# Two-layer flow backbone on one core: convolutions placed behind their columns, output sums read from PSUM, and VectorE kept in emission order through the global attention

## The chip, the cores and the metric

The kernel runs on one core of one Trainium2 chip. The metric is the device time of one execution in microseconds (us). A core has five engines that each work through a queue of their own: TensorE (PE; matmuls and, as PEld, their weight loads), VectorE (DVE), ScalarE (ACT), GpSimd (POOL) and SyncE (SP, which here only starts DMAs). Matmul results go to PSUM, in eight banks of 128 partitions x 2 KB; everything else on the chip lies in SBUF.

## The reference, cut to what matters

Two transformer-like layers run over 2048 latent tokens and 256 context tokens of width 1024. Each layer normalises (RMS, with shift and scale from a conditioning vector), projects to 3328 columns, mixes, multiplies by SiLU gates and projects back into the residual. All of it is float32.

```python
x = x + gate[:, None] * jnp.matmul(y, w_out[layer])
```

Layer 0 has two branches. Branch a is global attention with 8 heads over all 2304 keys:

```python
sc = jnp.einsum('bqkgd,bnkd->bkgqn', q_blk, k_all) * scale
p = jax.nn.softmax(sc, axis=-1)
o = jnp.einsum('bkgqn,bnkd->bqkgd', p, v_all)
```

Branch b is the Hyena operator: a short convolution of 3 taps over three parts of 512 channels, then twice a long convolution (through transforms of length 4096) times the next part:

```python
z = parts[0]
for o in range(HYENA_ORDER):
    z = parts[o + 1] * bidir_long_conv(z, filt[:, o, 0], filt[:, o, 1], d_skip[o])
```

The context tokens pass through the same weights and attend to themselves. Layer 1 has windowed attention (with a sink) and 2-D neighbourhood attention in place of the two branches. The output is the latent stream after layer 1.

## The kernel before

**How the order comes about.** The program is written as one long Python function, `kern`. Its instructions are handed to a scheduler that knows what each one reads and writes and that plays the program through with estimated durations; on each engine it takes, among the instructions that are ready in that play, the one written (emitted) first. The order found there is fixed in the queues, and on the chip each engine follows it strictly. Within `tc.manual_schedule(engines={...})` (L1474) the named engines keep the order of emission instead. Before, this held for TensorE alone in the global attention. Tiles come from pools: tiles of one tag share a ring of `bufs` slots, and a new tile waits until the slot's last user is through. A pool that is opened where another was closed waits for the tiles of the old one that lie in its memory.

**Precision.** A float32 product is made of three fast matmuls: both operands are split into a high part (`hi`) and the rest (`lo`), and `mm3` (L216) adds hi x hi, hi x lo and lo x hi. `load_w` (L229) loads a weight matrix in tiles of 128x512 (`wraw`, a ring of 3), has ScalarE cast each to `whi` (L242) and GpSimd subtract it to `wlo` (L243).

**Layer 0, first half (0 to about 1140 us).** The filters of Hyena and the modulation sums are made, and the tokens go through in three groups (`GRP`, L175): `ln0` normalises a group, `kvq` makes keys, values and queries, `us((b,))` makes column block b of the Hyena input for all three parts b (`cols`, evicted by VectorE at L341 and stored to `u0`), and `gates` the gate columns. The modulation of layer 0's gate and of layer 1 (`ada_sum`, L86, matmuls at L95) runs beside the second and third group and sums into three PSUM tiles of tag `x`, a ring of 3. In the third group stand, in this order: `us((0, 1))`, `conv(0)`, `us((2,))`, `conv(1)`, the first gate block, `gate_convs`, `kvq` and the second gate block with the first maxima. `conv(part)` calls `latent_conv` (L700): the short convolution of a part (VectorE at L725 and L726), transposes (L737), and for part 0 the first stage of the long convolution (matmuls at L668 and L669 into tiles of tag `x`).

**Global attention (about 1140 to 2255 us), `glob_attn` (L907).** 16 units (4 query blocks x 4 head pairs) of 9 batches, each batch 2 key tiles x 2 heads. A batch emits scores (L979, L980, exponentials on ScalarE at L981 into `Pt`, a ring of 5), then the products with the values of the batch before (L998) into one PSUM bank, and then GpSimd's running sum of probabilities (`pacc`, L993). Spread among the scores are the maxima of the coming unit: `max_step` emits a matmul (L892) into a bank of tag `m`, a ring of 3, and VectorE's reduction of it (L893); the 41st step of a unit, `max_fin`, collects them (L939, L943) and sends them by DMA into the queries. When a unit's last batch is through, `finish` (L1000) loads the gate (`agt`), sums the denominators (L1007), has ScalarE copy them (`rec`, L1009) and hands back six small steps, one of which follows each later score: four reciprocals of a quarter each (VectorE, L1012), two products on GpSimd (L1015, L1016) and `finish_y` (L365), which splits the result into `yhi` (ScalarE, L369) and `ylo` (L370) and stores both to `yT`.

**What else runs in it.** `hooks(b)` gives every batch further steps. Batches 0 to 109 carry the Hyena steps (`hyena_steps`, L754): for both orders 32 frequency steps and 16 inverse steps; the inverse step of order 0 multiplies in PSUM on VectorE, casts on ScalarE (L838) and subtracts on VectorE (L839). The very last step, in one piece, is 16 calls of `finish_y` on the result `yb` (L857 on), alternating between GpSimd and VectorE for the subtraction, with `yhi` and `ylo` both in the ring of 3 tiles of tag `hev`. At batch 110 the Hyena pools are closed and the pools of the output projection opened in their memory (`out_pools`, L1362); from batch 125 on one output job per batch follows (18 jobs; `job` in `out_jobs`, L1391). A job loads weights if it is the first of its half, loads `oy` (y transposed, hi and lo, rings of 2), loads `x` (`ox`, L1417 and L1419; 6 tiles in the first group), makes 24 matmuls (`pso`), multiplies them by the gate into the tile `ot` (L1425) and adds that to x (L1426). The context rows of modulation and the gate are handled the same way.

**Layer 1.** The attention's pools are closed (`stG`) and those of layer 1's projections opened on the same side (`hT1`, `s1`). For each of the three groups come the output jobs that are left, `norm` (transposes L302, activation L305 into `lnh`, L306 and L307), and `rows` and `cols`: window keys and values, window q, neighbourhood k and q, neighbourhood v, gates. In the third group `window_keys` (L1440) loads the keys and values of the window attention for all tokens (`wk1`, `wk2`, `wvt`, 4.5 MB) and its mask right behind the window q rows. Then come layer 1's attention (about 3080 to 3680 us) and the last output projection.

The two lines of a job that the change rewrites, and the call under the manual order:

```python
t = rg.tile([P, 512], F32, tag="bo", name="ot", bufs=3)
V.tensor_tensor(out=t, in0=po, in1=gate, op=ALU.mult)
V.tensor_tensor(out=x, in0=x, in1=t, op=ALU.add)
```

```python
with tc.manual_schedule(engines={mybir.EngineType.PE}):
    glob_attn(ga, gap, hooks, M0)
```

Of the kernel before, what the change touches and what calls it, by code (L numbers as in the profile page):

```python
# [9 lines left out]
F32 = mybir.dt.float32  # L10
# [30 lines left out]
def kern(ctx, tc, nc, I, C, out):  # L41
# [207 lines left out]
    class Proj:  # L249
# [98 lines left out]
        def ev_v(self, dst):  # L348
            def f(ps, tt):
                vt = self.rg.tile([P, 512], F32, tag="bo", name="vt", bufs=3)  # L350
                S.copy(vt, ps)
                nc.sync.dma_start(dst[tt], vt)
            return f
# [11 lines left out]
    def finish_y(sb, y, ft, t0, n, yT=yT, tags=("yhi", "ylo"), bufs=2, eng=None):  # L365

        hi = sb.tile([P, 512], F32R, tag=tags[0], name="yhi", bufs=bufs)
        lo = sb.tile([P, 512], F32R, tag=tags[1], name="ylo", bufs=bufs)
# [538 lines left out]
    def glob_attn(sb, ps, hooks, M0):  # L907
# [92 lines left out]
        def finish(n, yo, acc):  # L1000

            qb, hp = units[n]
            gt = sb.tile([P, 512], F32, tag="agt", name="agt", bufs=1)
# [4 lines left out]
            rec = sb.tile([P, 512], F32, tag="rec", name="rec", bufs=1)  # L1008
# [9 lines left out]
            return [lambda i=i: quarter(i) for i in range(0, 512, 128)] + [gate, lambda: finish_y(sb, yo, hp, qb * 512, 512, bufs=1, eng=G)]  # L1018
# [3 lines left out]
        acc, po, ended, last, pend = {}, {}, {}, None, []  # L1022
        total = 16 * 41
# [9 lines left out]
        for b in range(nb + 4):  # L1033
# [23 lines left out]
            if last is not None:  # L1057
# [5 lines left out]
                if ks == 16:  # L1063
                    yo = sb.tile([P, 512], F32, tag="yo", name="yo", bufs=2)
# [144 lines left out]
    with stS as st:  # L1209
# [109 lines left out]
        us((0, 1))  # L1319
# [6 lines left out]
        conv(0)  # L1326
        us((2,))
        conv(1)
# [52 lines left out]
    def out_jobs(g, halves, xs=None, early=()):  # L1381
# [9 lines left out]
        def job(b, i, tt, mm):  # L1391
            c = slice(512 * b, 512 * b + 512)
            rg, xo, gl = O0["rg"], O0["xo"], O0["gl"]
            if i == 0 and w_out.get("b") != b:
# [4 lines left out]
            ty = [xo.tile([P, 8, P], F32R, tag=f"oy{s}", name=f"oy{s}", bufs=2) for s in range(2)]  # L1399
            for s in range(2):  # L1400
                nc.sync.dma_start(ty[s].bitcast(F32), yT[s, :, :, tt * P:(tt + 1) * P].rearrange("f p t -> p f t"))
# [9 lines left out]
            else:  # L1411
                if len(xs) == i:
                    xt = xo.tile([P, 1024], F32, tag="lnx", name="ox", bufs=6)
                    if early:
# [9 lines left out]
            t = rg.tile([P, 512], F32, tag="bo", name="ot", bufs=3)  # L1424
            V.tensor_tensor(out=t, in0=po, in1=gate, op=ALU.mult)  # L1425
            V.tensor_tensor(out=x, in0=x, in1=t, op=ALU.add)  # L1426
# [13 lines left out]
    def window_keys():  # L1440
# [8 lines left out]
        wvt = aw.tile([P, 18, P], F32, tag="wv", name="wv")  # L1449
        for s in range(2):  # L1450
# [21 lines left out]

# [505 lines left out]
```

## Time and profile before

| what | value |
|---|---|
| median of 3 runs | 3856.79 us |
| lowest and highest | 3853.07 and 3857.14 us |
| the profiled execution's own time | 3855.73 us |
| its span, first to last instruction | 3854.0 us |
| mean granted TensorE clock | 0.975 |

The profile is one execution as the hardware profiler recorded it. Rows of the timeline give start, duration, engine, line, operation, output and inputs, shape and count, and in square brackets how long the engine was idle before and what it waited for. Rows that group a line's instructions give minimum, median and maximum in ns and the first and last start. Rows of the table by stretch give the busy time (and number of instructions) of each engine in a stretch, then the granted clock, the DMA share and GB/s; a table for one line names only that line's engine.

### The profile page before, as it was taken

How to read it: one execution, taken by the hardware profiler on the slowest of the kernel's cores; microseconds unless marked ns; L12 is line 12 of the kernel's file. 1: busy time of each engine (PE TensorE's matmuls, PEld its weight loads, DVE VectorE, ACT ScalarE, POOL GpSimd, SP SyncE). 2: the span in 40 equal slices, each digit the busy share in tenths (PEclk: the TensorE clock that was granted, in tenths of full speed). 3: DMA queues.
4: the chain of work that ended last, by engine and by line, in shares of the span. 5: the costliest groups of instructions: out<-in, count | busy, mean ns of one | idle time of the engine just before them, and what ended most of it. 6: DMA issues, size and time to landing. Idle time of an engine off the chain costs nothing.

```text
span 3854.0 us, 57179 instructions
## 1 busy us (share of the span) xinstructions
PE 3628.1 (94%) x20112; PEld 2607.1 (68%) x20112; DVE 2284.9 (59%) x4370; ACT 1784.9 (46%) x3480; POOL 1735.3 (45%) x1433
## 2 busy tenths in 40 slices
PE   6999999999779999999989989999999999999999
PEld 2788777666555544555545667778877888888887
DVE  5854862634967765776664348185168167677622
ACT  3644642423526655666452334344144266666610
POOL 1544642222447786777796554353244123222310
PEclk8999999999889999999999999999999999999999
DMA  6343445366666555443253545545566376365365
GB/s 195 118 140 123 133 133 141 114 224 219 203 191 189 172 162 173 123 148 110 91 197 96 146 148 152 164 152 155 157 175 169 118 171 147 90 151 135 113 178 169
DMA packets 537650, 586.23 MB, mean 152 GB/s; under 512 B 70590, under 2 KB 361720, under 8 KB 534290
## 3 DMA queue, kind: packets, MB, share of 16 engines
q1 hardware_dynamic: 521090, 551.10, 48.8%
q10 hardware_dynamic: 13856, 25.18, 1.8%
q0 software_dynamic: 2416, 6.29, 0.6%
q8 instruction: 159, 2.61, 0.3%
q14 instruction: 129, 1.06, 0.1%
HBM read 389.62 MB, written 192.75 MB: 151 GB/s over the span
## 4 chain that ended last, share of the span: by engine, by line
PE 69%; DVE 13%; issue 5%; DMA 5%; ACT 4%; POOL 2%; SPq 1%; ACTq 0%; DVEq 0%; POOLq 0%
PE psB L221 16%; PE pso L221 7%; PE po L998 6%; PE psA L221 5%; PE npt L1580 4%; PE no L1592 4%; PE pS L979 4%; PE pm L892 3%; PE pS L980 3%; PE ns L1561 2%; PE ns L1567 2%; DMA wraw<-in_w_in_dram 2%; PE hpX L806 1%; PE hpC L799 1%; PE hpH L811 1%
## 5 line engine op out<-in xcount | busy, mean ns | idle before, releaser
L243 POOL TENSOR_TENSOR wlo<-wraw,whi 128x512 fp32r<-128x512 f32 x368 | 494.4, 1357 | 784.9 <-ACT whi L242 529.3
L993 POOL TENSOR_TENSOR pacc<-pacc,Pt 128x512 f32<-128x512 f32 x512 | 647.1, 1286 | 191.4 <-ACT Pt L981 189.1
L221 PE MATMUL psB<-hT,whi 128*128 128x512 f32 (+1 forms) x2560 | 659.4, 346 | 3.9 <-DVE bo L341 3.5
L221 PE MATMUL psA<-whi,hT 128*128 128x512 f32 (+1 forms) x1952 | 574.8, 375 | 28.3 <-ACT vt L361 8.4
L893 DVE TENSOR_REDUCE mx<-pm 128x1 f32<-128x512 f32 (+1 forms) x640 | 389.1, 631 | 194.4 <-PE pm L892 190.1
L221 PEld LDWEIGHTS psB<-hT,whi 128*128 128x128 f32 x2560 | 445.1, 190 | 87.0 <-issue 23.9
L981 ACT ACTIVATE Pt<-pS 128x512 f32<-128x512 f32 x576 | 333.0, 597 | 352.5 <-PE pS L980 313.7
L221 PE MATMUL psB<-hT,wlo 128*128 128x512 f32 (+1 forms) x1280 | 433.8, 344 | 0.0
L221 PEld LDWEIGHTS psA<-whi,hT 128*128 128x128 f32 x1952 | 359.0, 194 | 98.7 <-ACT vt L361 11.7
L242 ACT CAST whi<-wraw 128x512 fp32r<-128x512 f32 x368 | 222.2, 618 | 301.4 <-DMA wraw<-in_w_in_dram 119.5
L221 PE MATMUL psA<-wlo,hT 128*128 128x512 f32 (+1 forms) x976 | 358.3, 372 | 0.9 <-POOL wlo L243 0.8
L221 PE MATMUL pso<-whi,oy 128*128 128x512 f32 x1088 | 343.2, 394 | 7.9 <-DMA oy<-yT 7.0
L979 PE MATMUL pS<-Q,K 128*128 128x512 f32 x576 | 330.9, 574 | 15.3 <-ACT Pt L981 14.9
L998 PE MATMUL po<-Pt,V 128*64 128x512 f32 x1152 | 283.0, 613 | 0.0
L221 PEld LDWEIGHTS psB<-hT,wlo 128*128 128x128 f32 x1280 | 242.4, 190 | 41.1 <-issue 10.8
L1580 PE MATMUL npt<-ident,np 128*128 128x128 f32 x1488 | 258.6, 283 | 3.4 <-DVE ggt L1157 1.9
L979 PEld LDWEIGHTS pS<-Q,K 128*128 128x128 f32 x576 | 109.7, 190 | 208.7 <-issue 95.3
L221 PEld LDWEIGHTS pso<-whi,oy 128*128 128x128 f32 x1088 | 205.2, 189 | 59.0 <-DMA oy<-yT 7.0
L980 PE MATMUL pS<-Q,K 65*128 65x512 f32 x576 | 231.3, 402 | 10.9 <-DMA Q<-mr 10.9
L892 PE MATMUL pm<-K,Q 128*128 128x512 f32 x600 | 217.0, 384 | 16.6 <-DVE mx L893 16.5
L221 PE MATMUL pso<-wlo,oy 128*128 128x512 f32 x544 | 213.2, 394 | 1.2 <-POOL wlo L243 1.2
L221 PEld LDWEIGHTS psA<-wlo,hT 128*128 128x128 f32 x976 | 189.9, 195 | 32.4 <-POOL wlo L243 3.1
(345 smaller groups left out, 6490.8 us busy)
## 6 DMA issues: line engine op xcount, KB each, us to landing
wraw<-in_w_in_dram SPq DMA_DIRECT2D x312, 256.0 KB
oy<-yT SPq DMA_DIRECT2D x72, 512.0 KB
qk<-tq SPq DMA_DIRECT2D x50, 512.0 KB
fA<-fev SPq DMA_DIRECT2D x64, 256.0 KB
adaw<-in_w_ada_dram SPq DMA_DIRECT2D x32, 512.0 KB
hxb<-XA SPq DMA_DIRECT2D x64, 256.0 KB
hfb<-fA SPq DMA_DIRECT2D x64, 256.0 KB
XC<-hevc ACTq DMA_DIRECT2D x64, 256.0 KB
```

The lines of the kernel that those rows point to most:

```text
L221: T.matmul(ps, a(x, kt), b(y, kt), start=(kt == 0 and n == 0), stop=(kt == 7 and n == 2))
L242: S.copy(hi, w)
L243: G.tensor_tensor(out=lo, in0=w, in1=hi.bitcast(F32), op=ALU.subtract)
L892: T.matmul(pm[:, :n], self.q1[:, h, qt * P:(qt + 1) * P], self.K1(c0, n), start=True, stop=True)
L893: V.tensor_reduce(out=self.mx[:, u, c:c + 1], in_=pm[:, :n], axis=AX.X, op=ALU.max)
L979: T.matmul(s, K1[kv][:, kt * P:(kt + 1) * P], q1[:, h, :], start=True, stop=False)
L980: T.matmul(s, K2[kv][:, kt * P:(kt + 1) * P], q2[:, h, :], start=False, stop=True)
L981: S.activation(pt[:, h, :], s, AF.Exp)
L993: G.tensor_tensor(out=acc[1][:, h], in0=acc[1][:, h], in1=p[:, h], op=ALU.add)
L998: T.matmul(po[64 * h:64 * h + 64, :], vt[:, kt, kv * 64:kv * 64 + 64], p[:, h, :], start=(kt == 0), stop=(kt == 17))
L1580: T.transpose(pt[:, i, :], self.p[h][:, (i0 + i) * P:(i0 + i + 1) * P], ident)
L1592: T.matmul(B["po"][64 * h:64 * h + 64, self.k, :], vt[:, kt, 64 * h:64 * h + 64], self.pT[h, i // 4][:, i % 4, :], start=(i == 0), stop=(i ...
```

## The change

Seven edits go together.

1. In the third group `conv(0)` stands right behind the columns of part 0, and `conv(1)` right behind those of part 1; the columns of part 2 follow.
2. In the global attention VectorE too keeps the order of emission, with all that the hooks emit there.
3. An output job loads `oy` before it loads weights and makes the gate.
4. In the first group's jobs from the third tile on, a one-column copy from the sum two jobs earlier into the new x tile makes the load of x wait for that sum.
5. A job multiplies in place in PSUM and adds x from there; the tile `ot` is gone.
6. The last unit's `agt`, `rec`, `yo`, `yhi` and `ylo` lie in three tiles of the `oy` rings instead of the attention's pool (`last_home`).
7. `window_keys` is called behind the neighbourhood v rows, and one-column copies from the last v tile into its three tiles make their loads wait for it.

```diff
@@ ev_v
-                vt = self.rg.tile([P, 512], F32, tag="bo", name="vt", bufs=3)
+                vt = self.late = self.rg.tile([P, 512], F32, tag="bo", name="vt", bufs=3)
@@ finish_y
-    def finish_y(sb, y, ft, t0, n, yT=yT, tags=("yhi", "ylo"), bufs=2, eng=None):
-        hi = sb.tile([P, 512], F32R, tag=tags[0], name="yhi", bufs=bufs)
-        lo = sb.tile([P, 512], F32R, tag=tags[1], name="ylo", bufs=bufs)
+    def finish_y(sb, y, ft, t0, n, yT=yT, tags=("yhi", "ylo"), bufs=2, eng=None, home=None):
+        hi = home[0] if home else sb.tile([P, 512], F32R, tag=tags[0], name="yhi", bufs=bufs)
+        lo = home[1] if home else sb.tile([P, 512], F32R, tag=tags[1], name="ylo", bufs=bufs)
@@ glob_attn, finish
-            gt = sb.tile([P, 512], F32, tag="agt", name="agt", bufs=1)
+            tail = iter(home[0]) if n == 15 else None
+            gt = next(tail) if tail else sb.tile([P, 512], F32, tag="agt", name="agt", bufs=1)
...
-            rec = sb.tile([P, 512], F32, tag="rec", name="rec", bufs=1)
+            rec = next(tail) if tail else sb.tile([P, 512], F32, tag="rec", name="rec", bufs=1)
...
-            ... finish_y(sb, yo, hp, qb * 512, 512, bufs=1, eng=G)]
+            ... finish_y(sb, yo, hp, qb * 512, 512, bufs=1, eng=G, home=home[1] if tail else None)]
@@ glob_attn, batches
                 if ks == 16:
-                    yo = sb.tile([P, 512], F32, tag="yo", name="yo", bufs=2)
+                    if m == 15:
+                        home[:] = last_home()
+                    yo = home[0].pop() if m == 15 else sb.tile([P, 512], F32, tag="yo", name="yo", bufs=2)
@@ third group
         ln0(2, xs2)
-        us((0, 1))
+        us((0,))
...
         conv(0)
+        us((1,))
+        conv(1)
         us((2,))
-        conv(1)
@@ job
             rg, xo, gl = O0["rg"], O0["xo"], O0["gl"]
+            ty = [xo.tile([P, 8, P], F32R, tag=f"oy{s}", name=f"oy{s}", bufs=2) for s in range(2)]
+            for s in range(2):
+                nc.sync.dma_start(ty[s].bitcast(F32), yT[s, :, :, tt * P:(tt + 1) * P].rearrange("f p t -> p f t"))
             if i == 0 and w_out.get("b") != b:
                 w_out["b"] = b
                 w_out["w"] = load_w(I['w_out'][0][:, c], 512)
             if g == 0 and i == 0:
                 gate_half(gl[:, c], mm("pg"), 0, 0, b)
-            ty = [xo.tile([P, 8, P], F32R, tag=f"oy{s}", name=f"oy{s}", bufs=2) for s in range(2)]
-            for s in range(2):
-                nc.sync.dma_start(ty[s].bitcast(F32), yT[s, :, :, tt * P:(tt + 1) * P].rearrange("f p t -> p f t"))
...
                     xt = xo.tile([P, 1024], F32, tag="lnx", name="ox", bufs=6)
+                    if g == 0 and i > 1:
+                        V.tensor_copy(xt[:, 0:1], xs[i - 2][:, 0:1])
...
-            t = rg.tile([P, 512], F32, tag="bo", name="ot", bufs=3)
-            V.tensor_tensor(out=t, in0=po, in1=gate, op=ALU.mult)
-            V.tensor_tensor(out=x, in0=x, in1=t, op=ALU.add)
+            V.tensor_tensor(out=po, in0=po, in1=gate, op=ALU.mult)
+            V.tensor_tensor(out=x, in0=po, in1=x, op=ALU.add)
@@ window_keys
-    def window_keys():
+    def window_keys(late):
...
+        for t in (wk1[:, 0, 0:1], wk2[:, 0:1], wvt[:, 0, 0:1]):
+            V.tensor_copy(t, late[:, 0:1])
@@ the global attention
+    def last_home():
+        ty = [O0["xo"].tile([P, 8, P], (F32, F32, F32R)[i], tag=f"oy{i % 2}", name="yl", bufs=2).rearrange("p a b -> p (a b)") for i in range(3)]
+        return [ty[0][:, :512], ty[0][:, 512:], ty[1][:, :512]], (ty[2][:, :512], ty[2][:, 512:])
...
-    with tc.manual_schedule(engines={mybir.EngineType.PE}):
-        glob_attn(ga, gap, hooks, M0)
+    with tc.manual_schedule(engines={mybir.EngineType.PE, mybir.EngineType.DVE}):
+        glob_attn(ga, gap, hooks, M0, last_home)
@@ layer 1, third group
-        if g == 2:
-            wm, sk, wk1, wk2, wvt = window_keys()
         pj.rows(1280, ...); pj.rows(768, ...); pj.rows(1792, 512, True, pj.ev_v(v1n))
+        if g == 2:
+            wm, sk, wk1, wk2, wvt = window_keys(pj.late)
```

More of the change, by code (lines that the diff above doesn't have):

```diff
@@ L905, in first_maxima, with glob_attn @@
         return Maxima(lambda c, n: ks[c // 1024][:, c % 1024:c % 1024 + n], q1, mx, bank)
-    def glob_attn(sb, ps, hooks, M0):
+    def glob_attn(sb, ps, hooks, M0, last_home):
         K1, K2 = [None] * 2, [None] * 2
@@ L1016, in gate @@
                 G.tensor_tensor(out=yo, in0=yo, in1=rec, op=ALU.mult)
-            return [lambda i=i: quarter(i) for i in range(0, 512, 128)] + [gate, lambda: finish_y(sb, yo, hp, qb * 512, 512, bufs=1, eng=G)]
+            return [lambda i=i: quarter(i) for i in range(0, 512, 128)] + [gate, lambda: finish_y(sb, yo, hp, qb * 512, 512, bufs=1, eng=G, home=home[1] if tail else None)]
         batches = [(n, kt) for n in range(16) for kt in range(0, 18, 2)]
@@ L1022, in glob_attn @@
         acc, po, ended, last, pend = {}, {}, {}, None, []
+        home = []
         total = 16 * 41
```

## The prediction

> **What bounds the kernel now.** I read the page first, then TensorE's waits over the whole run, then the busy times by stretch, and inside the stretches that the change touches the timelines of single engines.
>
> ```profile
> span 3854.0 us, 57179 instructions
> PE 3628.1 (94%) x20112; PEld 2607.1 (68%) x20112; DVE 2284.9 (59%) x4370; ACT 1784.9 (46%) x3480; POOL 1735.3 (45%) x1433
> PE lnpt L302 <- ACT lnh L305: 23.3, 9, 9.9
> PE pm L892 <- DVE mx L893: 17.8, 15, 4.3
> PE pS L979 <- ACT Pt L981: 14.9, 21, 6.2
> PE psA L221 <- ACT whi L242: 7.2, 3, 6.8
> PE pso L221 <- DMA oy<-yT: 7.0, 7, 2.9
> ```
>
> TensorE is busy 94% of the span. Only 226 us are to be had at all, and the change adds and removes no matmul. So the sum is made of TensorE's waits: who waits where, and what is late next. In a wait row stand total us, times, longest.
>
> ```profile
> 923.00:1070.00 147.00, 119.48 (x588) 89.64 (x585) 131.92 (x233) 76.92 (x146) 54.88 (x50) 0.89 0.67 213
> 1070.00:1140.00 70.00, 55.81 (x268) 43.65 (x269) 44.87 (x75) 15.79 (x30) 30.59 (x30) 0.82 0.75 210
> 1935.00:1960.00 25.00, 21.35 (x86) 10.58 (x85) 18.39 (x27) 15.10 (x28) 23.23 (x18) 1.00 0.50 186
> 1960.00:1984.00 24.00, 20.56 (x84) 10.22 (x83) 18.16 (x23) 12.95 (x23) 22.71 (x19) 1.00 0.53 190
> 1984.00:2010.00 26.00, 17.49 (x70) 9.39 (x69) 9.62 (x16) 10.47 (x19) 25.39 (x22) 0.92 0.97 293
> 2010.00:2048.00 38.00, 34.84 (x124) 16.85 (x123) 18.80 (x31) 16.07 (x29) 30.92 (x27) 0.88 0.17 56
> 2048.00:2063.00 15.00, 11.20 (x46) 7.03 (x44) 9.39 (x6) 2.56 (x5) 14.34 (x12) 1.00 0.27 72
> 2254.00:2290.00 36.00, 21.45 (x159) 20.03 (x159) 21.53 (x39) 16.75 (x31) 17.09 (x12) 0.86 0.47 153
> ```
>
> Columns: stretch, its length, busy PE, PEld, DVE, ACT, POOL, granted clock, DMA share, GB/s. Three limits show. From 923 to 1070 (the long convolutions' first half) VectorE is busy 131.9 of 147 us. From 1935 to 2063 (end of the Hyena steps, start of the output jobs) it is GpSimd, 116.6 of 128 us. From 2254 to 2290, behind the attention, nobody is busy: a hand-over.
>
> **Convolutions behind their columns.** Part 0 now stands ahead of the columns of part 1, and part 1 ahead of those of part 2. Whether that helps depends on what holds the convolutions. The rows are, in this order, the modulation matmuls of L95, the column evictions of L341 and the first-stage matmuls of L668:
>
> ```profile
> 900.00:923.00 23.00, 5.26 (x20) 0.72 (x20) 1.00 0.66 214
> ```
> ```profile
> 923.00:1140.00 217.00, 0.00 (x0) 0.86 0.70 212
> ```
> ```profile
> 923.00:1140.00 217.00, 15.67 (x32) 6.82 (x32) 0.86 0.70 212
> ```
>
> The three sums of the modulation hold all three PSUM banks of tag x until 923. All 32 matmuls of L668, which need one of these banks, come after that, and by then the last column block is evicted (no L341 left). So a bank holds the convolution, not its place behind the columns, and no fill is left to be handed over. I take 0 for this edit; bounds: 5 us lost by the new order of loads, 20 us won (half of the 27.5 + 14.2 = 41.7 us of idle TensorE).
>
> **Sums from PSUM.**
>
> ```profile
> 2038.86 23.48 POOL L993 TENSOR_TENSOR pacc<-pacc,Pt 128x512 f32<-128x512 f32 x19
> 2055.66 7.23 DVE L1426 TENSOR_TENSOR ox<-ox,ot 128x512 f32<-128x512 f32 x1
> 2063.55 0.39 PE L892 MATMUL pm<-K,Q 128*128 128x256 f32 x1 [4.35 <-DVE mx L893]
> ```
> ```profile
> L1425 DVE TENSOR_TENSOR ot<-pso,gl x32: 677/692/693, 2054.4 to 2826.7; 128x512 f32<-128x512 f32 x32
> ```
>
> The sum of two SBUF tiles took 7.23 us while GpSimd ran 19 additions without a gap, ended with them, and TensorE lost 4.35 us. The product with one input in PSUM took 0.69 in all 32 cases, the one of 2054.4 beside the same additions among them. The new sum has one input in PSUM: 4 us won (0 to 5).
>
> ```profile
> L780 DVE COPY yb<-hY x16: 144/144/154, 1159.3 to 1389.9; 128x1 f32<-128x1 f32 x16
> ```
>
> The new one-column copies, 4 in the jobs and 3 at the keys, cost 0.14 each by this row: nothing. The Trainium skill (SBUF — State Buffer, "Who interferes with whom") speaks against that: a copy within SBUF can be shut out for as long as a GpSimd instruction holds the port that the two share. That gives a rival below.
>
> **VectorE in the order of emission.** The win: reciprocals no longer run in a bunch ahead of the maxima.
>
> ```profile
> 1430.67 3.39 DVE L1012 RECIPROCAL rec<-rec 128x128 f32<-128x128 f32 x4 [3.65 <-ACT rec L1009]
> 1435.29 0.50 PE L892 MATMUL pm<-K,Q 128*128 128x512 f32 x1 [2.30 <-DVE mx L893]
> ```
>
> Four in a row (3.39 us) held the maxima, and TensorE waited 2.30 us. In emission order one reciprocal stands behind each score. Of the 17.8 us that TensorE waits for maxima 4.35 belong to the sums above; of the other 13.4 a good half, I assume, lies where GpSimd paces or stays. I take 5 us won (at most 13).
>
> The price: the last Hyena step emits 16 calls of `finish_y` in one place. Each is a ScalarE cast, a subtraction (8 on VectorE, 8 on GpSimd) and two stores, and all share a ring of three tiles, so that each waits for a store.
>
> ```profile
> 1936.07 0.62 ACT L369 CAST yhi<-yb 128x512 fp32r<-128x512 f32 x1 [0.33 <-DVE yb L855]
> 1939.89 1.18 DVE L370 TENSOR_TENSOR ylo<-yb,yhi 128x512 fp32r<-128x512 f32 x1 [2.08 <-DMA yT<-yhi]
> 1943.23 0.62 ACT L369 CAST yhi<-yb 128x512 fp32r<-128x512 f32 x1 [0.53 <-DMA yT<-ylo]
> 1979.95 0.62 ACT L369 CAST yhi<-yb 128x512 fp32r<-128x512 f32 x1 [0.70 <-DVE ylo L370]
> ```
> ```profile
> L370 POOL TENSOR_TENSOR ylo<-yb,yhi x8: 1266/1284/1297, 1936.8 to 1980.6; 128x512 fp32r<-128x512 f32 x8
> L370 DVE TENSOR_TENSOR ylo<-yb,yhi x8: 731/1242/4012, 1939.9 to 1975.9; 128x512 fp32r<-128x512 f32 x8
> ```
>
> In order, VectorE also waits for a ScalarE copy within each of the first order's 16 inverse steps; if the three banks of maxima did not hide that, it would cost 16 x 0.62, the cast's time, or 10 us: the other bound of the 5.
>
> Now the ring. The first tile, written at 1936.7, came free 3.2 us later; the next, ready at 1941.1, 2.2 us later. A chain of cast, subtraction (0.73 to 1.28) and store (2.2 to 3.2) is 3.6 to 5.1 us, two run side by side, so one call takes 1.8 to 2.6 us. Before, VectorE put maxima between its 8 subtractions. In the order of emission it can't: from the 2nd call to the 15th it is held for 13 such times, 23 to 33 us. Behind it queue all maxima of the following batches; TensorE fills three banks (some 3 us) and stops, for about 25 us; ScalarE's exponentials and GpSimd's additions stop behind it.
>
> What of this reaches the end is decided by GpSimd. In the stop it still has the 8 subtractions (10.3 us) and some 7 additions of 23.48 / 19 = 1.24 (8.7 us); of its 116.6 us 98 are left when TensorE goes on at about 1966. They end at 2064 without idle, at 2074 with the share of idle that it has now (11.4 in 128), against 2063 now. I take 8 us lost (bounds: 0, all made up; 41, nothing made up and the chain as long as now, 1939 to 1980).
>
> The Trainium skill (TensorE: Matmul & The Clock Gate, "What's actually happening") says that TensorE falls to half its clock after an idle window of about 3.4 us and needs as long a busy one to come back. By that the stop would cost 1.7 us more on resuming, an estimate from that page; the clock row 0.88 behind the waits of 2010 speaks for it.
>
> **Loads of the output jobs.** The oy tiles are asked for ahead of the weights, and from the third tile on x waits for the sum two jobs earlier.
>
> ```profile
> 2007.72 0.62 ACT L242 CAST whi<-wraw 128x512 fp32r<-128x512 f32 x1 [6.17 <-DMA wraw<-in_w_out_dram]
> ```
>
> ScalarE stood 6.17 us here with exponentials behind it, for a weight tile queued after six x tiles. With two x tiles ahead most of that goes, but in GpSimd's stretch: 2 us won (bounds 6 won; 3 lost, if x, asked for only as its product begins, arrives after it and VectorE holds maxima behind the sum). At the third group's first job oy landed late, 7.0 us over all jobs: 2 won (1 lost to 4 won).
>
> **The end of the attention.** The last unit's five tiles now lie in the output jobs' memory, so that the attention's pool comes free when its last sum is read. The tiles wait for oy slots of jobs that are long done.
>
> ```profile
> 2254.49 3.39 DVE L1012 RECIPROCAL rec<-rec 128x128 f32<-128x128 f32 x4 [10.62 <-ACT rec L1009]
> 2265.04 1.45 ACT L305 ACTIVATE lnh<-lnpt,gs 128x512 f32<-128x512 f32 x2 [3.77 <-DMA yT<-ylo]
> 2265.87 1.11 PE L302 MATMUL lnpt<-ident,ox 128*128 128x128 f32 x4 [9.89 <-ACT lnh L305]
> ```
>
> The next layer's first activation waited for the store of the last ylo, and TensorE 9.89 us for it. Now it can start at about 2255.2. Late next are VectorE's four reciprocals (until 2257.9) and GpSimd's last three steps ahead of the weight halves: 2 us stay. The granted clock of 0.86 over 36 us rises: 2 us. I take 10 won (6 to 14).
>
> **The window keys.** Their loads move from behind the q rows to behind the last v row.
>
> ```profile
> 2883.07 0.64 SPq L1452 DMA_DIRECT2D wk<-qk  x1
> 2897.89 9.08 DMA wraw<-in_w_in_dram
> 2900.00:2910.00 10.00, 3.20 (x9) 2.22 (x9) 4.38 (x7) 3.71 (x7) 4.17 (x4) 0.67 0.86 252
> ```
>
> Four key loads left from 2883; the weight tile of 2897.9 landed after 9.08 us, TensorE did 3.2 of 10 us of work and lost clock. The loads now meet the gate columns, where the weights are a block ahead. The three new copies wait on VectorE for that v tile, with evictions of gate columns queued behind them; SyncE's queue holds the last weight tiles behind the loads. The cover is the rest of that stage; if it is gone, the stall only moves. 8 won (3 to 12).
>
> **Sum**, in the order of the parts: 0 - 4 - 5 + 8 - 2 - 2 - 10 - 8 = -23 us. The profiled execution took 3855.73 us (1.73 around its span); it becomes 3832.7. The median, 3856.79, lies 1.06 higher: **3834 us**. About 0.2%, 8 us, is what a measurement can tell from no change.
>
> **Rivals.** (1) The convolutions do gain: half of the 41.7 us of idle, 20 us, gives 3814. For it: that idle is real. Against it: the bank row; chance 0.12. (2) The other side, slower: the block of `finish_y` isn't made up, because TensorE and not GpSimd ends the stretch. 41 instead of 8 gives 3867; it decides from a net price of 38.5 us on. For it: the chain ran 44 us. Against: GpSimd's 116.6 of 128; 0.15. (3) The change does not do what it says: the activation behind the attention waits for GpSimd's steps, the key loads shut out other weights, the waits for maxima stay. Then 5 instead of 10, 3 instead of 8 and 0 instead of 5 are won: 3849, the edge of no change; with half of rival 2 on top 3857; together 0.18. (4) The copies in the jobs are shut out as the 7.23 us sum was, each costing TensorE 4.35: 4 x 4.35 = 17 gives 3851. Against: GpSimd's back-to-back run ends at 2062, before the third job; 0.03. The forecast's own range, 3818 to 3848, holds 0.52.
>
> **How the numbers follow.** Faster: 0.52 + 0.12 + a little of rival 3 = 0.67. No change: 0.18. Slower: 0.15. The range 3808 to 3862 takes in rivals 1, 3 and 4 and leaves out most of rival 2.
>
> **What would show it.** Right: 8 subtractions of L370 on VectorE in a row at about 1940 with no maxima between, TensorE at a third in that slice; L1426 at 0.69 throughout; L305 starting some 3 us after the last denominator; no dip of TensorE at the key loads; L668 starting only after the last L95. Wrong: L668 earlier than L95's end, a longer way from 1936 to the first output job by over 20 us, or the next layer's first activation still waiting for a store.

## The result, and the profile after

The changed kernel takes 3875.74 us (median of 4 runs, 3874.85 to 3880.47), the kernel before 3855.57 (4 runs). The ratio is 1.0055, with a 95% interval from 1.0038 to 1.0073: it is **slower by 20 us** (0.55%). The forecast was 3834, 23 us faster than the median shown with it, and its range ended at 3862.

The page's first lines, and five of TensorE's larger waits (total us, times, longest):

```profile
span 3874.2 us, 57201 instructions
PE 3634.4 (94%) x20112; PEld 2607.1 (67%) x20112; DVE 2261.7 (58%) x4377; ACT 1786.0 (46%) x3480; POOL 1736.1 (45%) x1433
PE pm L892 <- DVE mx L893: 36.3, 13, 26.9
PE pmt L941 <- DVE nm L939: 22.3, 13, 3.0
PE lnpt L302 <- ACT lnh L305: 14.2, 10, 5.4
PE pS L979 <- ACT Pt L981: 10.2, 19, 3.0
PE pm L892 <- DMA Q<-q: 10.0, 1, 10.0
```

Before, the row of `nm` read

```profile
PE pmt L941 <- DVE nm L939: 11.8, 9, 2.3
```

Three rows say where the time went, and all three lie in the global attention: one wait of 26.9 us for a maximum, 22.3 us (11.8 before) for the reduction `nm` that closes a unit's maxima, and a wait of 10.0 us for a load of queries that TensorE never waited for before. Two of the other edits show as they should: the wait of `lnpt` fell from 23.3 to 14.2, and the 7.2 us of `psA` for `whi` are gone. The wait of `pS` fell too, from 14.9 to 10.2, but it is 9.3 in e1, which has none of the other edits.

To see in which stage the time lies, compare where the same instruction starts in the two traces: the first and the last score (L979), and the first ScalarE cast of the block of `finish_y` (L369). First the kernel before, then the changed one:

```profile
L979 PE MATMUL pS<-Q,K x576: 389/502/1327, 1127.7 to 2248.2; 128*128 128x512 f32 x192
L369 ACT CAST yhi<-yb x16: 607/618/622, 1936.1 to 1979.9; 128x512 fp32r<-128x512 f32 x16
```
```profile
L979 PE MATMUL pS<-Q,K x576: 387/502/1415, 1123.6 to 2285.3; 128*128 128x512 f32 x192
L369 ACT CAST yhi<-yb x16: 607/617/620, 1964.2 to 1997.5; 128x512 fp32r<-128x512 f32 x16
```

From the first score to that cast, the Hyena stage took 1936.1 - 1127.7 = 808.4 us and now takes 840.6. From the cast to the last score (the block and the output jobs) it was 312.1 and is 321.1. From the last score to the end of the span it was 1605.8 and is 1588.9. The changed kernel loses 32 us in a stage for which the forecast had a win of 5, loses 9 in the next, and wins 17 behind the attention. The same three lengths, in us, are given for each experiment below. Each is read from one traced execution, and stages with nothing changed in them still differ by 2 to 3 us between traces (the Hyena stage is 840.6 here and 838.2 in e5, and 805.1 to 808.4 in e2, e8, e10, e11 and e12); the medians are beside them. The part ahead of the first score varies by up to 8 us between traces, with no edit that explains it, so it is kept apart. The ratios are to the kernel before as timed beside each kernel (medians 3855.57, then 3857.23, 3856.08 and 3857.99).

| kernel | ratio to before (95%) | median us | before the scores | Hyena stage | block and jobs | behind |
|---|---|---|---|---|---|---|
| before | 1 | 3855.57 | 1127.7 | 808.4 | 312.1 | 1605.8 |
| changed | 1.0055 (1.0038 to 1.0073) | 3875.74 | 1123.6 | 840.6 | 321.1 | 1588.9 |
| e1_order_only | 1.0094 (1.0078 to 1.0110) | 3895.10 | 1128.4 | 831.4 | 331.4 | 1601.4 |
| e2_no_order | 0.9906 (0.9891 to 0.9921) | 3823.66 | 1125.2 | 806.4 | 298.7 | 1587.6 |
| e3_q_early | 1.0017 (1.0006 to 1.0028) | 3863.40 | 1128.8 | 823.4 | 322.2 | 1585.8 |
| e4_nm_early | 0.9993 (0.9984 to 1.0002) | 3857.08 | 1127.8 | 818.1 | 320.9 | 1589.8 |
| e5_rings | 1.0036 (1.0024 to 1.0048) | 3869.14 | 1125.2 | 838.2 | 311.0 | 1587.0 |
| e6_spread | 1.0025 (1.0014 to 1.0036) | 3866.27 | - | - | - | - |
| e7_order_mended | 0.9941 (0.9929 to 0.9953) | 3832.00 | 1125.0 | 803.3 | 308.4 | 1588.9 |
| e8_no_order_v | 0.9912 (0.9899 to 0.9925) | 3821.76 | 1127.0 | 805.1 | 297.4 | 1591.2 |
| e9_order_rings_v | 0.9913 (0.9899 to 0.9926) | 3823.69 | 1125.7 | 804.8 | 301.1 | 1591.0 |
| e10_even_jobs | 0.9945 (0.9933 to 0.9958) | 3837.63 | 1130.1 | 808.4 | 307.9 | 1589.4 |
| e11_conv_home_keys_back | 0.9943 (0.9929 to 0.9956) | 3837.34 | 1131.8 | 805.1 | 297.1 | 1601.7 |
| e12_sums_back | 0.9935 (0.9922 to 0.9947) | 3833.62 | 1130.5 | 805.2 | 308.4 | 1592.3 |

Two disturbed executions are left out, the profiled one of e6, whose trace is therefore not read, and one of e4.

**The three places.** First the load of the third unit's queries. It waits for two marker copies (L918, L924) from the second unit's maxima. Before, and then in the changed kernel, VectorE's copy, SyncE's issue of the load, and TensorE's reader:

```profile
1168.43 0.15 DVE L918 CAST Q<-mx 128x1 fp32r<-128x1 f32 x1
1169.07 0.55 SPq L919 DMA_DIRECT2D Q<-q  x1
```
```profile
1200.34 0.14 DVE L918 CAST Q<-mx 128x1 fp32r<-128x1 f32 x1
1201.26 0.38 SPq L919 DMA_DIRECT2D Q<-q  x1
1207.54 1.19 PE L892 MATMUL pm<-K,Q 128*128 128x512 f32 x2 [9.97 <-DMA Q<-q]
```

The maximum that the copy reads is there early in the second unit (e3, below, issues the load at 1171.5). The scheduler had run the copy then; in the order of emission it stands where it was written, right ahead of the first matmul that reads the load. A prefetch became a load on demand, and TensorE stood for 9.97 us.

Second the reduction `nm`. Before, then changed:

```profile
1654.97 0.20 DVE L939 TENSOR_REDUCE nm<-mx 128x8 f32<-128x40 f32 x1
1655.44 0.69 DVE L146 TENSOR_TENSOR cmW<-hpH,cmX 64x512 f32<-64x512 f32 x1 [0.27 <-PE hpH L811]
```
```profile
1676.97 0.68 DVE L146 TENSOR_TENSOR cmW<-hpH,cmX 64x512 f32<-64x512 f32 x1 [0.50 <-PE hpH L811]
1677.69 0.69 DVE L147 TENSOR_TENSOR cmW<-hpH,cmX 64x512 f32<-64x512 f32 x1
1678.49 0.70 DVE L148 TENSOR_TENSOR hpH<-hpH,cmt 128x512 f32<-128x512 f32 x1
1679.22 0.69 DVE L149 TENSOR_TENSOR hY<-hpH,cmW 128x512 f32<-128x512 f32 x1
1679.83 0.18 DVE L939 TENSOR_REDUCE nm<-mx 128x8 f32<-128x40 f32 x1
1680.07 0.38 PE L941 MATMUL pmt<-ident,nm 128*8 128x128 f32 x1 [2.74 <-DVE nm L939]
1680.37 3.30 PE L998 MATMUL po<-Pt,V 128*64 128x512 f32 x8
```

The reduction takes 0.2 us and all its maxima are there, but a Hyena spectrum step with four VectorE operations (L146 to L149) was emitted ahead of it. TensorE's transpose of `nm` comes next in TensorE's own order, so it waits 2.74 us, and here the eight products behind it take 3.30 us where they take 1.94 elsewhere. Five units have such a stop, of 2.74 to 3.02 us. Behind three of them, this one among them, the eight products take 3.28 to 3.68 us; behind the other two they take 1.94. By the starts of the same matmuls in e4, which has no such stop, one costs 4.4 to 4.9 us in the first case and 2.9 in the second.

Third the block of `finish_y`. VectorE's subtractions, the first maximum behind them, and TensorE's wait:

```profile
1968.30 0.88 DVE L370 TENSOR_TENSOR ylo<-yb,yhi 128x512 fp32r<-128x512 f32 x1
1972.79 1.74 DVE L370 TENSOR_TENSOR ylo<-yb,yhi 128x512 fp32r<-128x512 f32 x1 [3.61 <-POOL ylo L370]
...
1995.64 0.69 DVE L370 TENSOR_TENSOR ylo<-yb,yhi 128x512 fp32r<-128x512 f32 x1 [2.84 <-ACT yhi L369]
1996.26 2.21 DVE L893 TENSOR_REDUCE mx<-pm 128x1 f32<-128x256 f32 x4
1996.73 0.80 PE L892 MATMUL pm<-K,Q 128*128 128x512 f32 x1 [26.91 <-DVE mx L893]
```

This is the stop that the prediction described: 27.3 us from the first to the last subtraction, over 13 calls 2.1 us each, and no maximum between them.

### The profile page after: what moved, and what is told of

Same layout as the page of the kernel before. It is cut to its first block, busy times and chain, and to the rows that moved or that the text cites. A ratio compares the mean times of both kernels' runs of the same rounds, so it can differ in the third digit from the quotient of the medians.

```text
span 3874.2 us, 57201 instructions
## 1 busy us (share of the span) xinstructions
PE 3634.4 (94%) x20112; PEld 2607.1 (67%) x20112; DVE 2261.7 (58%) x4377; ACT 1786.0 (46%) x3480; POOL 1736.1 (45%) x1433
## 4 chain that ended last, share of the span: by engine, by line
PE 69%; DVE 13%; issue 5%; ACT 4%; DMA 4%; POOL 3%; SPq 1%; ACTq 0%; POOLq 0%; DVEq 0%
PE psB L221 16%; PE pso L221 9%; PE po L998 7%; PE npt L1593 5%; PE no L1605 4%; PE pS L979 4%; PE psA L221 4%; PE pm L892 3%; PE pS L980 3%; PE ns L1574 2%; PE ns L1580 2%; PE hpX L806 1%; DMA wraw<-in_w_in_dram 1%; PE hpC L799 1%; PE hpH L811 1%
## 5 line engine op out<-in xcount | busy, mean ns | idle before, releaser
L893 DVE TENSOR_REDUCE mx<-pm 128x1 f32<-128x512 f32 (+1 forms) x640 | 381.0, 628 | 221.5 <-PE pm L892 219.9
L221 PEld LDWEIGHTS psB<-hT,whi 128*128 128x128 f32 x2560 | 444.4, 190 | 85.9 <-issue 22.3
L979 PE MATMUL pS<-Q,K 128*128 128x512 f32 x576 | 329.6, 572 | 10.4 <-ACT Pt L981 10.2
L998 PE MATMUL po<-Pt,V 128*64 128x512 f32 x1152 | 291.7, 629 | 0.0
L221 PEld LDWEIGHTS psB<-hT,wlo 128*128 128x128 f32 x1280 | 242.3, 190 | 42.6 <-issue 13.4
L979 PEld LDWEIGHTS pS<-Q,K 128*128 128x128 f32 x576 | 109.2, 190 | 206.2 <-issue 99.4
```

The lines of the kernel that those rows point to most:

```text
L221: T.matmul(ps, a(x, kt), b(y, kt), start=(kt == 0 and n == 0), stop=(kt == 7 and n == 2))
L893: V.tensor_reduce(out=self.mx[:, u, c:c + 1], in_=pm[:, :n], axis=AX.X, op=ALU.max)
L979: T.matmul(s, K1[kv][:, kt * P:(kt + 1) * P], q1[:, h, :], start=True, stop=False)
L998: T.matmul(po[64 * h:64 * h + 64, :], vt[:, kt, kv * 64:kv * 64 + 64], p[:, h, :], start=(kt == 0), stop=(kt == 17))
```

## The experiments

Theory A was that the order of emission costs in these three places and that the other edits win. The rival was that the new waits in front of loads cost, and the order near nothing.

**The order alone, and all but the order.** e1 is the kernel before with one edit, e2 the changed kernel without it:

```diff
-    with tc.manual_schedule(engines={mybir.EngineType.PE}):
+    with tc.manual_schedule(engines={mybir.EngineType.PE, mybir.EngineType.DVE}):
```

> The kernel before with the second edit alone: VectorE keeps the order of emission in the global attention. Theory A (that order is what costs, in three places of the Hyena stage: the marker copies ahead of the second Q load 12 us, the reduction nm behind four spectrum operations some 4 us in each of four or five units, and the block of finish_y with some 7 to 10 net): 40 us slower than before, 3895 (3885 to 3905). Rival (the other six edits cost, for instance by the copies that make loads wait, and the order itself is near nothing): 3856, within 5 us of before.

> The changed kernel without the second edit: VectorE is ordered by the scheduler again in the global attention, all other edits stay. Theory A: 40 us faster than the changed kernel, some 3836, 20 us faster than before (15 to 25): end of the attention 7, window keys 8, sums and loads 4. Rival (the other edits cost): about 3876, no faster than the changed kernel.

e1: 3895.10, ratio 1.0094, as theory A had it. e2: 3823.66, ratio 0.9906 (0.9891 to 0.9921), some 35 us faster than before, and 12 below the 3836 expected. The rival falls. The order costs 38.6 us of span when it is alone (3892.6 - 3854.0) and 56.3 on top of the other edits (3874.2 - 3817.9; 52 by the medians, as the trace of e2 is of a quick execution): 34.2 in the Hyena stage and 22.4 in block and jobs. The other edits win 36.1: 13.4 in block and jobs and 18.2 behind the attention. The Hyena stage pays 34.2 with the other edits and 23.0 without them (e1), and most of that gap has a place: by the starts of the same matmuls, the changed kernel loses 6.4 us more than e1 at about 1456, where ScalarE stands 4.17 us for the split of a unit's result (L369) with exponentials queued behind it. In e1 that cast stands behind the exponentials and waits for nothing. The scheduler orders ScalarE and SyncE anew for each program, so this part need not be a price of VectorE's order: e1 and e3 have that order and do not pay it.

**The query load.** e3 emits it behind the 21st maximum of the second unit:

```diff
-            if k == 0 and u > 1:
+            if k == 0 and u > 2:
                 qs.append(load_q(*units[u]))
             if k < 40:
                 qs[u][2].step()
+                if u == 1 and k == 21:
+                    qs.append(load_q(*units[2]))
```

> The changed kernel, but the load of the third unit's queries with its two marker copies is emitted behind the 21st maximum of the second unit, not at the first maximum of the third. Theory A (in order, the marker copy stands where it is emitted, so the load starts when its first reader is due and TensorE waits 10.0 us for it, and 2.4 more at a lower clock behind that): 12 us faster than the changed kernel, 3863.5, and no wait of pm for Q in the trace. Rival (the load is late because the queue and the DMA engines are crowded there, or GpSimd's additions take over as the bound): at most 4 us faster, 3872 or more.

3863.40, ratio 1.0017, 12 us faster than the changed kernel, as theory A had it. The issue of the load is back to the middle of the second unit, and the wait of `pm` for it is in no row:

```profile
1171.50 0.37 SPq L919 DMA_DIRECT2D Q<-q  x1
```

The Hyena stage is 17.2 us shorter than in the changed kernel: 12.4 at this place by the starts of the same matmuls in both traces, the rest at 1456, where ScalarE no longer stands. That rest is not the load's price, since e1 loads as late and has no such stand.

**The reduction.** e4 emits it with the 40th maximum, one step ahead of its transpose:

```diff
             if k < 40:
                 qs[u][2].step()
+                if k == 39:
+                    nms[0] = max_nm(qs[u])
```

> The changed kernel, but the reduction nm of a unit's maxima is emitted with the 40th maximum, one step ahead of the transpose, not with the transpose. Theory A (nm stands behind the four VectorE operations of a spectrum step that wait for ScalarE, TensorE waits 2.7 to 3.0 us in five units and runs the next eight products at half rate): the five waits go, 15 us faster than the changed kernel, 3861 (3856 to 3866). Rival (the five waits only move to the next maximum, because the banks are full there anyway): 3 us faster at most, 3873 or more.

3857.08, ratio 0.9993 (0.9984 to 1.0002): level with before by this alone. The row that was 22.3 us in 13 waits reads now

```profile
PE pmt L948 <- DVE nm L940: 8.0, 8, 1.5
```

and the Hyena stage is 22.5 us shorter (the median falls by 18.7). Of that 14.3 is waiting for `nm`; by the starts of the same matmuls the five places make 19.5, the lower clock behind three of them included, and 3.3 lie behind 1456 again, where the clock is at half for 3.4 us instead of 10.2.

**The block.** e5 gives its `yhi` and `ylo` two rings of four tiles; e6 hands out one call behind each score of four batches; the output jobs still start at batch 125.

```diff
-  finish_y(sb, yb[...], 4 + ct, b * 512, 512, tags=("hev", "hev"), bufs=3, eng=(G, V)[(b + ct) % 2])
+  finish_y(sb, yb[...], 4 + ct, b * 512, 512, tags=("hxb", "hfb"), bufs=4, eng=(G, V)[(b + ct) % 2])
```
```diff
-            steps += [[[], [finish], []]] if o else [[[], [], []] for _ in range(3)]
+            steps += [[[], finish(ct), []] for ct in range(4)] if o else [[[], [], []] for _ in range(3)]
```

> The changed kernel, but yhi and ylo of the 16 calls of finish_y in one piece lie in two rings of four tiles (tags hxb and hfb, idle by then) instead of both in one ring of three. Theory A (VectorE is held by the chain of cast, subtraction and store through the ring; with four calls in flight the block is paced by GpSimd's eight subtractions, 8 x 1.26 = 10 us; and what the stop costs is GpSimd's idle time, some 20 us): the stop of 26.9 us falls to 10 to 13, the whole becomes 10 to 16 us faster than the changed kernel, 3860 to 3866. Prediction's own size (GpSimd makes most of the stop up, net price 8): at most 8 us faster, 3868 or more. Rival (the stores, not the ring, hold the block): the stop stays at 25 us or more, no change.

> The changed kernel, but the 16 calls of finish_y are spread, one behind each score of four batches, instead of one piece. Theory A (the block's net price is the 18 to 22 us in which GpSimd starves): no wait of pm of over 3 us there, 18 to 22 us faster than the changed kernel, 3854 to 3858. Prediction's own size (net price 8): 3866 to 3870. Rival (the ring holds each call anyway, so that VectorE is held as long in sum): no change.

e5: 3869.14, and its trace has a stop of 16.4 us instead of 26.9:

```profile
1986.19 0.79 PE L892 MATMUL pm<-K,Q 128*128 128x512 f32 x1 [16.39 <-DVE mx L893]
```

The stop is 10.5 us shorter, though longer than the 10 to 13 of theory A, the stage 10.1 shorter (321.1 to 311.0), the median 6.6. e6: 3866.27, 9 us faster than the changed kernel. Both medians lie nearer to the prediction's own size than to theory A, which had 18 to 22 for the spread; e7, below, puts the spread at 12.7 by its trace.

**All three mends.** e7 is the changed kernel with those of e3, e4 and e6.

> The changed kernel with three mends together: the early Q load, nm with the 40th maximum, and the spread finish_y. Theory A (these three places are the whole price of the order of emission): 12 + 18 + 20 = 50 us faster than the changed kernel less some 3 counted twice, 3826 to 3832, within 8 us of the kernel that keeps the other edits and lets the scheduler order VectorE (3824). Rival (in-order VectorE costs elsewhere too, by many small waits): 3845 or more.

3832.00, ratio 0.9941 (0.9929 to 0.9953). The Hyena stage takes 803.3 us, 37.3 less than in the changed kernel, where e3 and e4 make 17.2 + 22.5 = 39.7 singly, each with some us behind 1456 in it. With those two mends the stage pays nothing any more: 803.3, and 804.8 in e9, are level with the 805.1 to 808.4 of the scheduler's order. Block and jobs take 308.4, still 9.7 more than in e2.

e9 adds the rings of four and lets VectorE do all 16 subtractions:

> The changed kernel with the three mends, and in the spread finish_y also rings of four (hxb, hfb) and all 16 subtractions on VectorE. Theory A (what the mended order still loses against the scheduler's order, 10 us from 1940 to 2060, is VectorE held at single calls by the ring, waits of 3.8, 2.0 and 1.4 us, with GpSimd starved behind them): 6 to 10 us faster than the kernel with the three mends (3832), 3822 to 3826, no wait of pm over 1.5 us there. Rival (those 10 us are GpSimd's own work, or VectorE's subtractions now hold the maxima): 3829 to 3835.

3823.69, ratio 0.9913, as theory A had it; block and jobs take 301.1. No maximum is waited for over 1 us there; one score waits 4.07 us for an exponential. So the block's price in the changed kernel, 321.1 - 298.7 = 22.4 us, splits by these traces into 12.7 for standing in one piece, 7.3 for the ring of three and GpSimd's half of the subtractions, and 2.4 left. The order of emission, mended in all places, is as fast as the scheduler's (e2), not faster; both beat the kernel before by 0.9%.

**What GpSimd has to do with it.** Busy times of PE, PEld, DVE, ACT, POOL over block and jobs, for the changed kernel (the stop, then the whole stretch), and for e2:

```profile
1968.50:1996.70 28.20, 1.32 (x6) 0.72 (x4) 7.23 (x10) 9.16 (x16) 13.46 (x11) 0.59 0.62 229
```
```profile
1963.00:2098.00 135.00, 102.35 (x394) 53.17 (x395) 63.98 (x102) 57.56 (x101) 110.09 (x91) 0.87 0.38 129
```
```profile
1931.00:2046.00 115.00, 102.89 (x389) 52.63 (x388) 64.83 (x100) 54.66 (x100) 109.82 (x90) 0.94 0.45 148
```

GpSimd does the same work in both, 110 us. In e2 it is idle for 5 us of 115, in the changed kernel for 25 of 135, 14.7 of them in the stop. The two stretches differ by 20 us, and GpSimd's idle time by as much. But so does TensorE's, which has 102 to 103 us of work in both, so these rows alone do not say that GpSimd sets the price. What they do show is how little of its work GpSimd did in the stop, 13.46 us.

Two attempts to change what GpSimd has to do there. e8 is e2 with all 16 subtractions of the block on VectorE; e10 is e2 with the 18 jobs spread over batches 116 to 143.

```diff
-        elif b >= NH + 15 and jobs:
+        elif b >= NH + 6 and jobs and (b - NH - 6) * 18 // 28 < (b - NH - 5) * 18 // 28:
```

> The kernel with all edits but VectorE's order of emission, and all 16 subtractions of the block of finish_y on VectorE instead of 8 on GpSimd. Theory A (GpSimd bounds 1931 to 2046, 109.8 of 115 us busy): 8 x 1.26 = 10 us less for GpSimd, 6 to 10 us faster than without this edit, 3814 to 3818. Rival (TensorE or the store chain is the bound there): no change, 3822 to 3826.

> The kernel with all edits but VectorE's order of emission (3824), and the 18 output jobs of the attention spread evenly over batches 116 to 143, two in three, instead of one in each from batch 125 to 142. Theory A (behind the Hyena steps GpSimd's running sum paces the batches, TensorE is idle 12 of 115 us from 1931 to 2046, and later TensorE paces them): 5 to 10 us faster, 3814 to 3819. Rival (the weights and x of the first job, asked for earlier, meet the stores of finish_y, and the job's wlo adds to GpSimd's work where it is the bound): no change or slower, 3822 to 3830.

e8: 3821.76, ratio 0.9912 against 0.9906, no change; the stage is 1.3 us shorter. Ten us less for GpSimd won nothing, so GpSimd's work alone was not the bound. The trace shows TensorE waiting for VectorE instead, which is held by the subtractions (2.63 us for a maximum at 1954, 2.84 for `nm` at 1970); that this used up the ten us is likely, but not shown. e10: 3837.63, 14 us slower than e2. GpSimd, which I meant to feed, ran dry:

```profile
1985.00:2060.00 75.00, 65.19 (x242) 39.47 (x238) 27.92 (x50) 23.13 (x39) 55.15 (x45) 0.86 0.62 188
2005.23 0.79 PE L221 MATMUL pso<-whi,oy 128*128 128x512 f32 x1 [3.76 <-ACT whi L242]
```

It is busy 55 of 75 us there: the matmuls of a job stand in TensorE's order ahead of the scores, and the first of them waits 3.76 us for its weights. Theory A fell for both.

**The other edits.** e11 undoes three of them in e2, each in a stage of its own (convolutions behind their columns, `last_home`, place of the window keys); e12 puts the tile `ot` back.

> The kernel with all edits but VectorE's order of emission (3824), with three further edits undone, each in a stage of its own: the order of columns and convolutions, the last unit's tiles in the output jobs' memory, and the place of the window keys. Theory A (as the stages of the traces show): 0 in 923 to 1140, 6.5 back at the end of the attention, 8 to 9 back at 2880 to 2960; 15 us slower, 3839. Rival 1 of the prediction (the convolutions do gain): 5 us or more slower in 923 to 1140 too.

> The kernel with all edits but VectorE's order of emission (3824), with the tile ot and the sum of two SBUF tiles put back in the output jobs. Theory A (the sum beside GpSimd's additions takes some 7 us once and holds the maxima): a sum of over 5 us at about the second job, 4 us slower, 3828. Rival (the 12 us won from 1984 to 2063 came from the order of the loads alone): no change, within 1 us in that stage.

e11: 3837.34, 14 us slower than e2, and the part behind the attention is 14.1 longer: by the starts of the same matmuls some 5.7 at the end of the attention, 4 at about 2400 and 7.7 at the key loads, less 3 in small steps. Both waits of before are back, behind the attention and at the weights behind the key loads:

```profile
2251.44 1.11 PE L302 MATMUL lnpt<-ident,ox 128*128 128x128 f32 x4 [9.74 <-ACT lnh L305]
2890.27 1.22 PE L221 MATMUL psA<-whi,hT 128*128 128x512 f32 x2 [6.78 <-ACT whi L242]
```

The part ahead of the scores ends at 1131.8 in e11, and at 1127.7 and 1128.4 in the two other traces with the old order of the convolutions (before and e1); in the ten with the new order it ends between 1123.6 and 1130.5. The means lie 2.4 us apart, less than the spread of either: a gain of that size can't be told from none, and 20 us are ruled out. e12: 3833.62, 10 us slower than e2; block and jobs take 308.4, 9.7 more. One sum takes over 7 us again, and TensorE waits behind it. By the starts of the same matmuls this place costs 7.5 us, the wait of 4.31 and then products of 0.63 us in place of 0.39, at a granted clock of 0.61 over 8 us:

```profile
2048.73 7.19 DVE L1433 TENSOR_TENSOR ox<-ox,ot 128x512 f32<-128x512 f32 x1
2056.57 0.58 PE L892 MATMUL pm<-K,Q 128*128 128x256 f32 x1 [4.31 <-DVE mx L893]
```

## Why the prediction was wrong

**VectorE in the order of emission, waits for maxima: -5, between -13 and +10. This step failed.** With the other edits in place it costs 34.2 us in the Hyena stage. The step asked only whether VectorE's maxima would come later. It named the two things that the order moves there, reciprocals and the splits of the first order, and found them small, which they are: with the two mends the stage is level with the scheduler's order, neither 5 us better nor 10 worse. What it did not ask is what else VectorE does between the maxima that somebody waits for. The marker copies of the query load (12.4 us at their place, by e3) and `nm` (19.5 at its five places, by e4) were in the code and in the trace of before, both run well ahead of where they are emitted. The trace of before had the row to look for: `nm` at 1654.97, ahead of the four operations emitted before it.

**The block of `finish_y`: +8, between 0 and +41.** The mechanism was right to the number: 23 to 33 us of hold (27.3), TensorE stopped for 25 (26.9), some 2 us a call (2.1). The term that was mis-sized is what GpSimd makes up. The step gave GpSimd 19 us of work in the stop; it had 13.46 of 28.2, as its own subtractions wait in the same chain. And it took GpSimd's idle share of before as what stays, where without the block the changed loads and sums leave it 5 us in 115. Measured 22.4, within the bounds.

**Rival 2 against what happened.** It ended on the right side and within 9 us of the median (3867), but for a part of the reason: the block paid 22.4 where it needed 38.5, and the larger share came from the Hyena stage, which was in no rival. So its nearness is luck for the most part. (The prediction's 3857 for rival 3 with half of rival 2 does not come out either: half of 41 instead of 8 is 16.5 us, which gives 3866.)

**Sums from PSUM: -4, between 0 and -5.** Measured 9.7 by the stage and 7.5 at the sum itself (e12), more than the bound. The step counted TensorE's wait of 4.35 us alone and put what follows it at nothing: in e12 TensorE ran at a granted clock of 0.61 for 8 us behind the wait, and ScalarE and GpSimd did nothing in these 8 us. The new sum ran as said, 0.69 in all cases:

```profile
L1432 DVE TENSOR_TENSOR ox<-pso,ox x30: 690/691/692, 2095.9 to 2854.9; 128x512 f32<-128x512 f32 x30
```

**Loads of the output jobs: -2.** The 13.4 us that the other edits win in block and jobs less the sums' 9.7 leave 3.7, within the bounds but not far above the 2 to 3 us between traces. The wait of `oy` at the third group's first job did not get smaller (4.15 after, 2.93 before): that -2 did not come.

**End of the attention: -10.** L305 now starts 2.1 us behind the copy of the last denominators:

```profile
2290.92 0.59 ACT L1010 COPY yl<-pd 128x512 f32<-128x512 f32 x1 [0.77 <-PE pd L1008]
2292.97 1.45 ACT L305 ACTIVATE lnh<-lnpt,gs 128x512 f32<-128x512 f32 x2
2298.70 1.27 ACT L242 CAST whi<-wraw 128x512 fp32r<-128x512 f32 x2 [4.28 <-DMA wraw<-in_w_in_dram]
```

The wait of 9.89 us is gone. The next layer then runs into its weights (4.28), and into waits of 2.4 and 1.5 us for its first normalised columns; by e11 the edit is worth some 5.7 us, a little under the lower bound of 6.

**Window keys: -8.** The loads leave at 3034.5 now, behind the last weights of the v rows, and the row of `psA` waiting for `whi` is gone. With them back the wait is 6.78 us and the place takes 7.7 more (e11). Right.

**Convolutions: 0.** The last matmul of L95 starts at 917.6 and the first of L668 at 919.8: as said, they start only when the banks are free. Rival 1 is out. Rival 4 too: the copies took 0.14 us each, in the jobs and at the keys.

Some 4 to 5 us at about 2400, in layer 1's second group, are won in the changed kernel, in e1 and in e2, and about 2 of them in e11. No edit touches that place; what sets them is open. They do not change the verdict.

## What to carry to other kernels

When an engine is put into the order of emission, walk through all that it does in that stretch, not only its bulk work. Look for short instructions that release something: marker copies ahead of a prefetch, a last small reduction ahead of a transpose. The trace of before shows them running ahead of instructions emitted earlier, and each must be emitted where it is to run. A burst of calls that share a small ring is one long instruction to an engine in order; hand it out in pieces, or give it a ring as long as its store takes. And when you price a stop by the work that other engines can go on with, look whether that work waits in the same chain: GpSimd did 13.5 us in a stop that was to give it 19. Count too what the clock takes behind the stop.

## What the runs showed of the hardware

A short stop can cost more than its length. After 2.74 us without a matmul (to 1680.07) TensorE ran its next eight products in 3.30 us instead of 1.94, with a granted clock of 0.60 over those 4 us. Behind the next such stop, also of 2.74 us (to 1752.50), nothing of the kind is seen:

```profile
1676.00:1680.00 4.00, 1.32 (x5) 0.42 (x3) 3.28 (x6) 2.87 (x6) 3.00 (x4) 0.97 0.69 184
1680.00:1684.00 4.00, 3.93 (x11) 1.20 (x12) 0.29 (x2) 0.00 (x0) 2.09 (x3) 0.60 0.05 17
1752.50:1756.50 4.00, 4.00 (x16) 1.84 (x17) 0.97 (x2) 0.66 (x2) 2.42 (x4) 1.00 0.03 7
```

Of the five short stops at `nm`, three paid in this way. So did the 2.30 us at 1435 in the kernel before: the clock is 0.59 from 1435 to 1439. What decides shows in the clock records of the traces. The granted clock changes only at points that lie a multiple of 3.41 us apart, and what counts is how long TensorE idled between two of these points. In the 13 traces that are read here, from 1150 to 2240 us, the clock fell to half behind all 72 such steps of full clock with over 1.85 us of idle, behind none of 3732 with under 0.84, and behind 31 of 175 in between. The five stops put 2.20, 1.71, 2.43, 1.68 and 2.39 us into one step, and the second and fourth, which fall more evenly on two steps, paid nothing. The Trainium skill (TensorE: Matmul & The Clock Gate, "What's actually happening") puts the fall to half clock behind at least one idle window of about 3.4 us. The length of the window agrees; but it need not be idle throughout, and there the measurement decides: 1.85 us of idle in it were enough.

Behind the stop of 26.9 us the granted clock was 0.69 over 6.3 us, which is 2.0 us lost; the prediction's estimate from that page of the Trainium skill, 1.7, agrees.

The sum of two SBUF tiles took 7.23 us in the kernel before and 7.19 in e12, each time while GpSimd ran its additions without a gap, and ended 0.55 us behind the last of them; with one input in PSUM it took 0.69. The Trainium skill (SBUF — State Buffer, "Who interferes with whom") says that a VectorE instruction with two SBUF inputs contends with a GpSimd instruction that reads SBUF; the runs agree, and show that one sum can be held for five to six additions of 1.24 us in a row.
